# Head projections in two halves of 384 weight columns instead of three units of 256, with other ring sizes, on one core

## The chip, the cores and the metric

The program runs on one core of one Trainium2 chip. The metric is the device time of one execution in microseconds; of the kernel before there are three runs. The profile's own execution is a fourth, and its times count from its first instruction.

## What is computed

One step of a hybrid decoder layer for 512 prompt tokens and 8 x 4 sample tokens, width 1024. The part that the change touches is the input projection of the four attention heads and what is done with it:

```python
z_q, z_k, z_v, z_conv, z_mq, z_gate = split_combined(h @ lw['w_in'])
q, k, v = attention_qkv(z_q, z_k, z_v, pos, lw)        # norm of each head vector, rotary on 32 of 128 dims
for g, (window, dilation) in enumerate(((128, 1), (512, 4), (2048, 16))):
    o, l = dilated_band_attention(q[:, :, g * 4:(g + 1) * 4], k, v, window, dilation)
a = combine_dilated(outs, lses).reshape(B, S, ATTN_WIDTH) @ lw['w_attn_proj']
m = memory_branch(z_mq, mem_k, mem_v, lw)              # attention of normed z_mq over 256 memory tokens
out = merge_branches(z_gate, a, conformer, m, lw['w_out'])
y = x1 + hier_moe(rms_norm(x1))                        # 32 experts, top 1 group, top 2 in it
```

Each head h thus has six vectors of 128 per token out of `w_in`: Q0, Q1, Q2 (one for each window), K, V and MQ (the query into the memory). The weights are float32; the kernel multiplies them in three passes of a rounded high part and a low part.

## The kernel before

The stages follow each other: memory keys and values (`mem_kv`), the four heads, three convolution units (`glu`), the sample tokens' attention, the branches and gates, the output projection, the router, and 32 experts. Within the heads the code is written as `project_head(0)`, then for each h `attend_head(h)` and `project_head(h + 1)`. A scheduler then sets the order of the instructions on each engine, and each engine keeps to its order.

**Projection.** A head's weights come as three units of 256 columns (`cols_h`: Q0 Q1, then Q2 K, then V MQ), each a 1 MB block of a ring in SBUF. `split` makes the high part by a cast on ACT (L231) and the low part by a subtraction on DVE (L232), into the pool `whl`. For each unit the four blocks of 128 tokens are multiplied by `mm_nat` (L238 to L240, 24 matmuls of 256 columns each, called projection matmuls here), and two blocks share a PSUM tile of `mm`, which has three tiles. Then `norm_vecs` squares on ACT (L368), takes the root on POOL (L370, L371) and scales on DVE (L373); `rope` rotates on POOL; TensorE transposes (L441, L460) into a tile of `tr`, and a copy brings the result to `T`. `sample()` (L400 to L414) multiplies the 32 sample tokens by all three units and uses one `mm` tile and one `tr` tile; its last copy, on ACT (L406), needs DVE's norm.

**Attention.** For each of four query blocks: scores (L480 to L488) from the Qs and K, exp (L492), transposes (L498, L499), copies (L501 on DVE, L502 on ACT), values (L505, L508), a scaling on ACT (L510), a transpose (L512) and a copy (L513, ACT). Then twice, for the memory: scores (L518), exp (L525), scaling (L529), transposes (L533), a copy (L535, DVE), values (L538), a copy (L540, ACT). The pool `tr` has two PSUM tiles, and they go round in the order of the code: `attend_head(h)` takes all its turns before the transposes of `project_head(h + 1)`.

**Loads.** SP issues the weight loads; a load waits until its block is free and, by its semaphore, until the transfer eight issues before it has landed. The expert stage takes its 1 MB blocks from several pools in turn: `ring` 6, `ring2` 4, `ring2b` 2, `ring2c` 1, `ring3` 4, `ring4` 2, `ring5` 2, together 21; a load (L573) waits for the matmuls that read the block before: gate (L1477, `pg`), up (L1477, `pu`) and down (L1495, `pd`). An expert has six blocks.

## Time and profile before

| | before |
|---|---|
| runs, us | 1236.84, 1236.11, 1234.14 |
| median, us | 1236.11 |
| profiled execution, span, us | 1233.3 |
| PE busy, us (share) | 1157.4 (94%) |
| DVE, ACT, POOL busy, us | 483.4, 302.5, 290.2 |

The span is what the profile records from the first to the last instruction; the profile gives no time for what lies around it, and the median of the three runs is 2.8 us above the span. A busy engine has an instruction under way; PE is TensorE's matmuls. In the rows further down, a time stands from the span's start.

### The profile page before, as it was taken

To read this page: it belongs to the slowest core of one execution; us is meant where nothing else is said; L and a number is where in the kernel's file an instruction comes from. 1 tells how busy PE (TensorE), PEld (TensorE's weight loads), DVE (VectorE), ACT (ScalarE), POOL (GpSimd) and SP (SyncE) were. 2 spreads that over 40 slices of the span, in tenths; PEclk is the share of its full clock that TensorE was granted. 3 is DMA by queue.
4 is the path that set the end of the run, shared out by engine and by line. 5 is a ranking of instruction groups with operands and counts; after the bars stand their busy time and mean duration, and the time that the engine had idled before them with its cause. 6 is when DMAs were issued, how large, how long until landed. Compare 5 with 4: busy or idle time off the path is not lost. (4 is left out here: it accounts for less than half of the span.)

```text
span 1233.3 us, 22282 instructions
## 1 busy us (share of the span) xinstructions
PE 1157.4 (94%) x9248; PEld 850.2 (69%) x9250; DVE 483.4 (39%) x959; ACT 302.5 (25%) x731; POOL 290.2 (24%) x472
## 2 busy tenths in 40 slices
PE   6999999999999989999999988999999998898884
PEld 6898898989546889999998844555555554444441
DVE  6644434443635879856432263112142121111110
ACT  7434343422322422144332231000000000000000
POOL 5443434530840730213221000111111111111001
PEclk9999999999999989999999998999999999999998
DMA  9995754133647542312328487999999999999994
GB/s 319 228 330 153 228 164 139 43 108 103 239 137 266 184 150 69 103 44 95 137 74 358 154 305 297 388 394 399 401 393 400 397 394 401 403 407 401 402 399 145
DMA packets 125575, 313.02 MB, mean 254 GB/s; under 512 B 12842, under 2 KB 69490, under 8 KB 108833
## 3 DMA queue, kind: packets, MB, share of 16 engines
q1 hardware_dynamic: 115440, 295.58, 64.1%
q0 software_dynamic: 7280, 14.36, 5.2%
q10 hardware_dynamic: 2752, 1.65, 0.5%
q8 instruction: 74, 1.21, 0.4%
q14 instruction: 29, 0.23, 0.1%
HBM read 295.66 MB, written 31.35 MB: 265 GB/s over the span
## 5 line engine op out<-in xcount | busy, mean ns | idle before, releaser
L1499 POOL DMA_INDIRECT out_y_all<-work,ids x32 | 49.6, 1549 | 459.9 <-DVE work L1498 420.3
L664 PE MATMUL mm<-hTh,lo 128*128 128x272 f32 x512 | 148.6, 292 | 0.0
L662 PE MATMUL mm<-hTh,hi 128*128 128x272 f32 x512 | 148.6, 290 | 0.0
L663 PE MATMUL mm<-hTl,hi 128*128 128x272 f32 x512 | 148.5, 290 | 0.0
L1477 PE MATMUL pu<-w,xgT 128*64 128x256 f32 x992 | 115.6, 381 | 17.9 <-DMA w<-in_w_expert_up 16.6
L1495 PE MATMUL pd<-w,work 128*64 128x512 f32 x512 | 119.7, 609 | 1.4 <-DMA w<-in_w_expert_down 1.4
L1477 PE MATMUL pg<-w,xgT 128*64 128x256 f32 x992 | 115.0, 380 | 4.1 <-DMA w<-in_w_expert_gate 2.8
L1477 PEld LDWEIGHTS pu<-w,xgT 128*64 128x64 f32 x992 | 69.1, 137 | 61.2 <-DMA w<-in_w_expert_up 26.6
L238 PE MATMUL mm<-hi,hTh 128*128 128x256 f32 x384 | 110.2, 287 | 0.0
L239 PE MATMUL mm<-lo,hTh 128*128 128x256 f32 x384 | 110.0, 286 | 0.0
L240 PE MATMUL mm<-hi,hTl 128*128 128x256 f32 x384 | 109.8, 286 | 0.0
L1477 PEld LDWEIGHTS pg<-w,xgT 128*64 128x64 f32 x992 | 70.3, 137 | 55.7 <-issue 16.7
L232 DVE TENSOR_TENSOR lo<-w,hi 128x2048 fp32r<-128x2048 f32 (+2 forms) x46 | 82.2, 1803 | 45.9 <-ACT hi L231 45.8
L1486 DVE TENSOR_TENSOR work<-work,pu 128x256 f32<-128x256 f32 x32 | 13.5, 421 | 216.1 <-PE pu L1477 216.1
L662 PEld LDWEIGHTS mm<-hTh,hi 128*128 128x128 f32 x512 | 96.8, 189 | 1.8 <-ACT aS L896 0.8
L663 PEld LDWEIGHTS mm<-hTl,hi 128*128 128x128 f32 x512 | 97.0, 190 | 0.3 <-issue 0.2
L664 PEld LDWEIGHTS mm<-hTh,lo 128*128 128x128 f32 x512 | 96.5, 189 | 0.6 <-issue 0.5
L683 DVE SCALAR_TENSOR_TENSOR cT<-u,cT 128x512 f32<-128x512 f32 x120 | 89.8, 766 | 1.7
L1495 PEld LDWEIGHTS pd<-w,work 128*64 128x64 f32 x512 | 34.4, 139 | 65.1 <-issue 60.1
L1296 PE MATMUL px<-h,ohs 128*64 128x512 f16 x620 | 74.0, 380 | 5.6 <-DVE gates L1373 2.8
L231 ACT CAST hi<-w 128x2048 fp32r<-128x2048 f32 (+2 forms) x50 | 68.0, 1389 | 28.1 <-PE mm L663 24.7
L999 POOL TENSOR_TENSOR z<-z,gth 128x272 f32<-128x272 f32 x32 | 35.7, 1117 | 164.4 <-DVE gth L998 164.4
(452 smaller groups left out, 2114.1 us busy)
## 6 DMA issues: line engine op xcount, KB each, us to landing
w<-in_w_expert_gate SPq DMA_DIRECT2D x64, 1024.0 KB, 11.1
w<-in_w_expert_up SPq DMA_DIRECT2D x64, 1024.0 KB, 10.3
w<-in_w_expert_down SPq DMA_DIRECT2D x64, 1024.0 KB, 11.2
w<-in_w_in SPq DMA_DIRECT2D x30, 512.0 KB, 7.1
w<-in_w_in SPq DMA_DIRECT2D x12, 1024.0 KB, 6.9
out_k_win_sample<-in_cache_k SPq DMA_DIRECT2D x8, 1016.0 KB, 12.7
out_v_win_sample<-in_cache_v SPq DMA_DIRECT2D x8, 1016.0 KB, 14.8
w<-in_cache_k SPq DMA_DIRECT2D x6, 1024.0 KB, 5.8
```

Source lines behind the costliest of these rows:

```text
L231: nc.scalar.copy(hi[:, s], v8(t)[:, s])
L232: last_lo[0] = e.tensor_tensor(lo[:, s], v8(t)[:, s], hi[:, s].bitcast(F32), op=ALU.subtract)
L238: nc.tensor.matmul(ps, xh[k], wh[k], start=(k == 0), stop=False)
L239: nc.tensor.matmul(ps, xh[k], wl[k], start=False, stop=False)
L240: nc.tensor.matmul(ps, xl[k], wh[k], start=False, stop=(k == n - 1))
L662: nc.tensor.matmul(ps, wh[k], xh[k], start=(k == 0), stop=False)
L663: nc.tensor.matmul(ps, wh[k], xl[k], start=False, stop=False)
L664: nc.tensor.matmul(ps, wl[k], xh[k], start=False, stop=(k == n - 1))
L683: nc.vector.scalar_tensor_tensor(cTf[:, c, :NP], u[:, c, j:j + NP], w, cTf[:, c, :NP], op0=ALU.mult, op1=ALU.add)
L1296: nc.tensor.matmul(px[CAP * f:CAP * f + CAP], oh[:, i, :], src[:, 4 * f:4 * f + 4, :], start=(i == GORD[0] and r == 0), stop=(i == GORD[-1 ...
L1477: last = nc.tensor.matmul(ps[CAP * f:CAP * f + CAP], xT[:, k, :], ws[k // 4][:, k % 4, 256 * f:256 * f + 256], start=(k == 0), stop=(k == 7))
L1495: last = nc.tensor.matmul(pd[CAP * f:CAP * f + CAP], hT[:, kk % 2, CAP * (kk // 2):CAP * (kk // 2) + CAP], w[4 + kk // 2][:, kk % 2, 512 * ...
```

## The change

`project_head` makes two passes over the token blocks, each with 384 weight columns: half 0 takes all of unit 0 and the first 128 columns of unit 1 (Q0, Q1, Q2), half 1 the rest of unit 1 and all of unit 2 (K, V, MQ). The new `split3` writes the high and low parts of a half into tiles of 384 columns; they make `whl` larger, and the six blocks of `ring3`, which stand in its place later, use that room. A PSUM tile of `mm` now holds one token block of a half. There are 768 projection matmuls of 384 columns where there were 1152 of 256. `sample()` of head 0 stands at the start of half 1. The ring has five blocks instead of six, `ring3` six instead of four, so the expert stage has 22 instead of 21. The scratch for DMA descriptors is 4 KB. Lines of the changed file are shifted: L238 is L253, L368 L383, L400 L415, L406 L421, L413 L428, L510 L520, L512 L522, L513 L523, L525 L535, L533 L543, L535 L545, L538 L548, L540 L550; the transposes of the queries are now L468, those of K and MQ L461.

```diff
@@ -47,14 +47,14 @@
 
 TCKW = dict(schedule_with_timeline_sim=True)
 
-RING = 6
+RING = 5
 RING2 = 4
 RING2B = 2
 RING2C = 1
-RING3 = 4
+RING3 = 6
 RING4 = 2
 RING5 = 2
-SPOS = 2
+SPOS = 4
 NPG = 2
 COJ = 1
 WK = {4: "hi", 5: "lo"}
@@ -65,7 +65,7 @@
 DEPTH = 4
 NBUSY = (50, 4)
 GORD = (4, 0, 1, 2, 3)
-ORD3 = (0, 3, 1, 2)
+ORD3 = (0, 4, 5, 1, 2, 3)
 AHJ = 1
 NGH = 3
 MVT = {0: "hi"}
@@ -230,6 +230,21 @@
             s = slice(q * n, q * n + n)
             nc.scalar.copy(hi[:, s], v8(t)[:, s])
             last_lo[0] = e.tensor_tensor(lo[:, s], v8(t)[:, s], hi[:, s].bitcast(F32), op=ALU.subtract)
+        return hi, lo
+
+    def split3(units, half, n):
+        hi = whl.tile([P, 8, 384], F32R, name=nm("hi"), tag="hi")
+        lo = whl.tile([P, 8, 384], F32R, name=nm("lo"), tag="lo")
+        if half == 0:
+            parts = ((units[0], 0, 0, 256), (units[1], 0, 256, P))
+        else:
+            parts = ((units[1], P, 0, P), (units[2], 0, P, 256))
+        for q in range(n):
+            ks = slice(q * 8 // n, (q + 1) * 8 // n)
+            for t, c, d, w in parts:
+                src = v8(t)[:, ks, c:c + w]
+                nc.scalar.copy(hi[:, ks, d:d + w], src)
+                nc.vector.tensor_tensor(lo[:, ks, d:d + w], src, hi[:, ks, d:d + w].bitcast(F32), op=ALU.subtract)
         return hi, lo
 
     def mm_nat(ps, xh, xl, wh, wl):
@@ -385,9 +400,9 @@
     ropec = rope_t[:, 0:P].rearrange("p (i c) -> p i c", i=4)
     ropes = rope_t[:, P:2 * P].rearrange("p (i c) -> p i c", i=4)
 
-    def bc4(v, ip):
+    def bcn(v, ip, n):
         w = v[:, 2 * ip:2 * ip + 2, :]
-        return w.unsqueeze(2).to_broadcast([P, 2, 2, 32])
+        return w.unsqueeze(2).to_broadcast([P, 2, n, 32])
 
     def project_head(h, units):
         T = t_tile(nm("T")).bitcast(F32).rearrange("p (s t) -> p s t", s=5)
@@ -413,52 +428,47 @@
                 nc.tensor.transpose(psT[:, c * 96:(c + 1) * 96], sA[:96, c, :], ident[:96, :96])
             nc.vector.tensor_copy(Ts[:, h].rearrange("p a q -> p (a q)"), psT[:, :192])
 
-        for u in range(3):
-            wh, wl = split(units[u], H0ENG if h == 0 else (nc.vector,))
-            for ip in range(2):
-                if u * 2 + ip == (SPOS if h == 0 else 0):
+        al = slice(None)
+        for half in range(2):
+            wh, wl = split3(units, half, 2 if h == 0 else 1)
+            for i in range(4):
+                if half * 4 + i == (SPOS if h == 0 else 0):
                     sample()
-                ps = mm.tile([P, 2, 2, HD], F32, name=nm("mm"), tag="mm")
-                for i2 in range(2):
-                    i = 2 * ip + i2
-                    s = slice(i * P, (i + 1) * P)
-                    mm_nat(ps[:, i2], [hTh[:, k, s] for k in range(8)], [hTl[:, k, s] for k in range(8)],
-                           [wh[:, k, :] for k in range(8)], [wl[:, k, :] for k in range(8)])
-                A = hs_.tile([P, 2, 2, HD], F32, name=nm("A"), tag="A", bufs=3)
-                al = slice(None)
-                if u < 2:
-                    ix = [(al, i2, s_, al) for i2 in range(2) for s_ in range(2)]
-                    gg = [gq, gq if u == 0 else gk] * 2
-                    norm_vecs(ps, A, [(x, x) for x in ix], gg, P)
-                    rope(A, bc4(ropec, ip), bc4(ropes, ip), [P, 2, 2])
-                    if u == 1:
-                        nc.gpsimd.dma_start(
-                            O["k_win_prompt"][0, 0, ip * 256:(ip + 1) * 256, h, :].rearrange("(i p) d -> p i d", p=P),
-                            A[:, :, 1, :])
+                ip, i2 = i // 2, i % 2
+                ps = mm.tile([P, 3, HD], F32, name=nm("mm"), tag="mm")
+                s = slice(i * P, (i + 1) * P)
+                mm_nat(ps.rearrange("p s d -> p (s d)"), [hTh[:, k, s] for k in range(8)],
+                       [hTl[:, k, s] for k in range(8)], [wh[:, k, :] for k in range(8)], [wl[:, k, :] for k in range(8)])
+                if i2 == 0:
+                    A = hs_.tile([P, 2, 3, HD], F32, name=nm("A"), tag="A", bufs=3)
+                if half == 0:
+                    norm_vecs(ps, A, [((al, v), (al, i2, v)) for v in range(3)], [gq] * 3, P)
+                else:
+                    nc.scalar.copy(vh[:, i, :], ps[:, 1, :])
+                    VENG.dma_start(vp[32 * i:32 * i + 32], vh[:, i, :])
+                    norm_vecs(ps, A, [((al, 2 * v), (al, i2, v)) for v in range(2)], [gk, gmq], P)
+                if i2 == 0:
+                    continue
+                nv = 3 - 2 * half
+                rope(A[:, :, :nv], bcn(ropec, ip, nv), bcn(ropes, ip, nv), [P, 2, nv])
+                if half:
+                    nc.gpsimd.dma_start(
+                        O["k_win_prompt"][0, 0, ip * 256:(ip + 1) * 256, h, :].rearrange("(i p) d -> p i d", p=P),
+                        A[:, :, 0, :])
                     pt = tr.tile([P, 2, 2, P], F32, name=nm("tr"), tag="tr")
-                    for i2 in range(2):
-                        for s_ in range(2):
-                            nc.tensor.transpose(pt[:, i2, s_, :], A[:, i2, s_, :], ident)
-                    dst = T[:, 2 * u:2 * u + 2, ip * 256:(ip + 1) * 256].rearrange("p s (i t) -> p s i t", i=2)
-                    for s_ in range(2):
-                        dv, sv = dst[:, s_], pt[:, :, s_]
-                        if (u, s_) != (1, 1):
-                            dv = dv.rearrange("p i (r a) -> p i r a", r=4)
-                            sv = sv.rearrange("p i (a r) -> p i r a", r=4)
-                        if u == 0:
-                            nc.scalar.copy(dv, sv)
-                        else:
-                            nc.vector.tensor_copy(dv, sv)
-                else:
-                    nc.scalar.copy(vh[:, 2 * ip:2 * ip + 2, :], ps[:, :, 0, :])
-                    for i in range(2 * ip, 2 * ip + 2):
-                        VENG.dma_start(vp[32 * i:32 * i + 32], vh[:, i, :])
-                    ix = [(al, i2, 1, al) for i2 in range(2)]
-                    norm_vecs(ps, A, [(x, x) for x in ix], [gmq, gmq], P)
-                    pt = tr.tile([P, 2, P], F32, name=nm("tr"), tag="tr")
-                    for i2 in range(2):
-                        nc.tensor.transpose(pt[:, i2, :], A[:, i2, 1, :], ident)
-                    nc.scalar.copy(T[:, 4, ip * 256:(ip + 1) * 256].rearrange("p (i t) -> p i t", i=2), pt)
+                    for j in range(2):
+                        for v in range(2):
+                            nc.tensor.transpose(pt[:, j, v, :], A[:, j, v, :], ident)
+                    dst = T[:, 3:5, ip * 256:(ip + 1) * 256].rearrange("p s (i t) -> p i s t", i=2)
+                    (nc.scalar.copy if ip else nc.vector.tensor_copy)(dst, pt)
+                    continue
+                for j in range(2):
+                    pt = tr.tile([P, 3, P], F32, name=nm("tr"), tag="tr")
+                    for v in range(3):
+                        nc.tensor.transpose(pt[:, v, :], A[:, j, v, :], ident)
+                    q0 = (2 * ip + j) * P
+                    dst = T[:, 0:3, q0:q0 + P].rearrange("p s (r a) -> p s r a", r=4)
+                    (nc.scalar.copy if j else nc.vector.tensor_copy)(dst, pt.rearrange("p s (a r) -> p s r a", r=4))
         nc.gpsimd.dma_start(O["v_win_prompt"][0, 0, :, h, :].rearrange("(i p) d -> p i d", p=P), vh)
         return T, vh, vp
 
@@ -1627,7 +1637,7 @@
     from concourse.bass_utils import run_bass_kernel_spmd
 
     arrs, cols = _consts()
-    nc = bacc.Bacc("TRN2", target_bir_lowering=False, num_devices=1)
+    nc = bacc.Bacc("TRN2", target_bir_lowering=False, num_devices=1, dynamic_dma_scratch_size=4096)
     arrays, ins, outs = {}, {}, {}
     named = [(k, np.ascontiguousarray(inputs[k])) for k in _INS] + list(zip(_CONSTS, arrs))
     for k, a in named:
```

TensorE, end of the attention of head 1, as it stood before. `tr` tiles are the attention's, `mm` tiles those of the projection of head 2 (`hi`, `lo` weights, `hTh` tokens), `P` the probabilities of the memory part, `sA` the sample tile.

```order
L512 MATMUL tr_1984<-ident,PT_1973 128x128 [waits Activation_49]
L533 MATMUL tr_2000<-ident,P_1992 128x128 [waits PE_49]
...
L239 MATMUL mm_2324<-lo_2245,hTh 128x256
...
L238 MATMUL mm_2404<-hi_2400,hTh 128x256
...
L538 MATMUL tr_2007<-PT_2005,mv 128x256 [waits DVE_49,Activation_49]
...
L533 MATMUL tr_2024<-ident,P_2016 128x128 [waits PE_49]
...
L239 MATMUL mm_2404<-lo_2401,hTh 128x256
...
L538 MATMUL tr_2031<-PT_2029,mv 128x256 [waits DVE_49,Activation_49]
...
L413 MATMUL tr_2090<-ident,sA_2073 128x96 [waits PE_49,Pool_49]
...
L239 MATMUL mm_2470<-lo_2401,hTh 128x256
```

The rows left out between these are projection matmuls of head 2 or further transposes of the same group: 5 and 22 of them stand between the first transposes of L533 and the first L538, 26 and 7 between the second ones, and 23 follow the transposes of L413 before anything that waits.

The same place now. `mm_2226` is the last tile of the projection of head 2, `mm_2539` the first of head 3, `A` the normed queries of head 2.

```order
L255 MATMUL mm_2226<-hi_2098,hTl 128x384
...
L518 MATMUL tr_1802<-vp_1252,PT_1799 32x128 [waits DMAHW0_49,Activation_49]
...
L522 MATMUL tr_1810<-ident,PT_1799 128x128 [waits Activation_49]
L543 MATMUL tr_1826<-ident,P_1818 128x128 [waits PE_49]
...
L548 MATMUL tr_1833<-PT_1831,mv 128x256 [waits DVE_49,Activation_49]
...
L543 MATMUL tr_1850<-ident,P_1842 128x128 [waits PE_49]
...
L548 MATMUL tr_1857<-PT_1855,mv 128x256 [waits DVE_49,Activation_49]
...
L428 MATMUL tr_1918<-ident,sA_1901 128x96 [waits PE_49,Pool_49]
...
L468 MATMUL tr_2000<-ident,A_1947 128x128 [waits Activation_49,Pool_49]
...
L468 MATMUL tr_2005<-ident,A_1947 128x128 [waits DVE_49]
...
L253 MATMUL mm_2539<-hi_2487,hTh 128x384 [waits Activation_49]
```

Left out are 24 sample matmuls of head 3 (L415, between the first two rows shown), score masks, the transposes of the last block, and repeats of the rows shown; no projection matmul stands between the first row and the last.

ACT at that place now: the squares of the last projection tile, the high parts for half 1 of head 3, then the attention's copies and exponentials.

```order
L447 COPY vh_1868<-mm_2226 128x128 [waits PE_49]
L383 ACTIVATE sq_2254,hms_2253<-mm_2226 128x128 [waits Pool_49]
L246 CAST hi_2715<-w_2278 128x8x128 [waits DMAHW4_49]
L246 CAST hi_2715<-w_2281 128x8x256 [waits DMAHW2_49,DMAHW1_49]
L448 DMA vp_1869<-vh_1868 32x4x128 [waits DMAHW0_49,Activation_49]
L383 ACTIVATE sq_2254,hms_2253<-mm_2226 128x128 [waits Activation_49]
L523 COPY aT_613<-tr_1773 128x4x32 [waits PE_49]
L535 ACTIVATE P_1842,den_1841<-S_1837,m_1840 128x256 [waits PE_49]
L535 ACTIVATE P_1842,den_1841<-S_1837,m_1840 128x256
L512 COPY PT_1799<-tr_1795 128x128 [waits DVE_49]
```

Before, the cast of a unit stood between squares of earlier tiles, with projection matmuls still to come on TensorE; now both casts of a half stand behind the last projection tile of the head and ahead of four operations of the attention's tail.

SP's order of loads at the start, before. `w_195`, `w_198` and `w_201` are the three units of head 0, `w_193` the last unit of the memory keys and values; `cf`, `gmq`, `cm` and `br` stand for twenty small loads.

```order
L219 DMA w_193<-in_w_mem_kv 128x8x256 [waits DMAHW0_49]
L219 DMA w_195<-in_w_in 128x8x128 [waits DMAHW1_49]
L581 DMA cf<-in_constf 128x306 [waits DMAHW3_49]
...
L593 DMA gmq<-in_mq_norm_g 128x128 [waits DMAHW7_49]
...
L219 DMA w_198<-in_w_in 128x8x128 [waits DMAHW3_49,DVE_49,Pool_49]
...
L600 DMA cm<-in_constm 128x1504 [waits DMAHW0_49]
...
L652 DMA br<-in_b_router_expert 128x32 [waits DMAHW0_49]
L219 DMA w_201<-in_w_in 128x8x128 [waits DMAHW1_49,DVE_49,Pool_49]
```

The same place now.

```order
L219 DMA w_193<-in_w_mem_kv 128x8x256 [waits DMAHW0_49]
L591 DMA cf<-in_constf 128x306 [waits DMAHW1_49]
...
L603 DMA gmq<-in_mq_norm_g 128x128 [waits DMAHW5_49]
...
L219 DMA w_195<-in_w_in 128x8x128 [waits DMAHW3_49,DVE_49,Pool_49]
...
L610 DMA cm<-in_constm 128x1504 [waits DMAHW6_49]
...
L662 DMA br<-in_b_router_expert 128x32 [waits DMAHW6_49]
L219 DMA w_198<-in_w_in 128x8x128 [waits DMAHW7_49,DVE_49,Pool_49]
...
L219 DMA w_201<-in_w_in 128x8x128 [waits DMAHW1_49,DVE_49,Pool_49]
```

The first unit now stands behind ten small loads, and the second, which half 0 needs too, stands behind all twenty, next to the third.

## Rows read from the trace of the kernel before

**Rows 1.** The page: busy time (share of the span), and one costly group.

```profile
PE 1157.4 (94%) x9248; PEld 850.2 (69%) x9250; DVE 483.4 (39%) x959; ACT 302.5 (25%) x731; POOL 290.2 (24%) x472
...
L1499 POOL DMA_INDIRECT out_y_all<-work,ids x32 | 49.6, 1549 | 459.9 <-DVE work L1498 420.3
```

**Rows 2.** Windows: length, busy us (count) by engine, PEclk, DMA share, GB/s.

```profile
60.00:300.00 240.00, 240.00 (x2184) 213.41 (x2176) 99.62 (x258) 94.64 (x332) 94.45 (x174) 1.00 0.52 164
740.00:1018.00 278.00, 267.39 (x2060) 144.00 (x2058) 66.81 (x148) 22.77 (x43) 29.53 (x19) 0.99 1.00 385
1018.00:1233.00 215.00, 173.26 (x1264) 85.62 (x1264) 31.84 (x58) 11.06 (x23) 20.05 (x13) 0.98 0.94 366
```

**Rows 3.** Timeline of PE: start, length, instruction; 48 steps between the second and third row.

```profile
42.87 0.28 PE L238 MATMUL mm<-hi,hTh 128*128 128x256 f32 x1
...
76.93 0.28 PE L238 MATMUL mm<-hi,hTh 128*128 128x256 f32 x1
...
82.63 0.28 PE L238 MATMUL mm<-hi,hTh 128*128 128x256 f32 x1
...
564.94 0.28 PE L662 MATMUL mm<-sh,ph 128*128 128x272 f32 x1
...
567.94 0.29 PE L663 MATMUL mm<-hTl,hi 128*128 128x272 f32 x1
```

**Rows 4.** Timeline of PE: an attention tail and sample matmuls, projection rows left out.

```profile
125.94 0.60 PE L533 MATMUL tr<-ident,P 128*128 128x128 f32 x4
...
129.59 1.02 PE L538 MATMUL tr<-PT,mv 128*128 128x256 f32 x4
...
130.45 0.60 PE L533 MATMUL tr<-ident,P 128*128 128x128 f32 x4
...
204.70 1.49 PE L400 MATMUL mm<-w,hTs 128*32 128x256 f32 x18
```

**Rows 5.** ACT by line and shape, 140 to 260 (last row 30 to 45).

```profile
L231 ACT CAST hi<-w 128x2048 fp32r<-128x2048 f32 x7 | 13.3, 1900 | 0.0
L368 ACT ACTIVATE sq<-mm 128x128 bf16<-128x128 f32 x42 | 11.7, 279 | 2.3 <-PE mm L240 1.7
...
L525 ACT ACTIVATE P<-S,m 128x256 f32<-128x256 f32 x8 | 3.7, 471 | 0.0
...
L513 ACT COPY aT<-tr 128x128 f32<-128x128 f32 x8 | 3.1, 388 | 21.0 <-PE tr L512 21.0
...
L510 ACT ACTIVATE PT<-tr,m 128x128 f32<-128x128 f32 x8 | 2.9, 368 | 11.4 <-PE tr L508 11.3
...
L231 ACT CAST hi<-w 128x1024 fp32r<-128x1024 f32 x4 | 4.0, 1048 | 0.0
```

**Rows 6.** DVE by line and shape, 140 to 260.

```profile
L232 DVE TENSOR_TENSOR lo<-w,hi 128x2048 fp32r<-128x2048 f32 x7 | 16.1, 2293 | 10.2 <-ACT hi L231 10.2
...
L373 DVE SCALAR_TENSOR_TENSOR A<-mm,hrs,gq 128x128 f32<-128x128 f32 x26 | 8.0, 344 | 16.5 <-PE tr L441 8.8 <-POOL hrs L371 7.7
...
L535 DVE COPY PT<-tr 128x512 f32<-128x512 f32 x4 | 2.8, 688 | 4.4 <-PE tr L533 4.4
```

**Rows 7.** DMA issues of SP in time, then landing of the pair at 33.28.

```profile
17.75 6.96 SPq L219 DMA_DIRECT2D w<-in_w_in  x2
...
33.28 1.02 SPq L219 DMA_DIRECT2D w<-in_w_in  x2
...
45.51 14.54 SPq L219 DMA_DIRECT2D w<-in_w_in  x8
...
DMA to landing us min/median/max: 4.1/4.8/5.4
```

**Rows 8.** DMA issues of SP, expert weights.

```profile
736.66 13.90 SPq L573 DMA_DIRECT2D w<-in_w_expert_gate  x2
...
843.19 3.25 SPq L573 DMA_DIRECT2D w<-in_w_expert_gate  x2
...
943.21 4.01 SPq L573 DMA_DIRECT2D w<-in_w_expert_gate  x2
```

## The prediction

> **What bounds the kernel now.** The page's busy times come first: PE is busy for 1157.4 us of the span of 1233.3 [rows 1]. The windows by stage say what that share hides. [...] From 740 on the DMA share is 1.00, and from 1018 PE works only 173 of 215 us: there the expert weights set the end [rows 2]. Their issue by SP shows where this begins: the pair of gate loads at 736.66 takes 13.90 us, since its second load waits for a block; from 750.6 on load follows load, and the six experts between the gate loads at 843.19 and those at 943.21 are 36 blocks of 1 MB in 100.0 us, 2.78 each [rows 8]. The loads up to there are limited by how many blocks are free, the rest by the DMA.
>
> A shift of the heads is passed on in full: SP's loads at 736.66 wait for the expert matmuls, and these follow the heads on the same engine. The end is then the time of that wait plus the blocks still to be loaded.
>
> **The matmuls.** The page's mean of a projection matmul is its latency; what counts is the distance from start to start. 48 steps of 256 columns take 82.63 − 76.93 = 5.70 us, 0.1188 each; 24 steps of 272 columns take 567.94 − 564.94 = 3.00, 0.1250 each [rows 3]. So 16 columns more cost 6.2 ns, 0.39 a column; and 0.1188 less 256 × 0.39 leaves some 19 ns that do not depend on the columns. [...] Before: 1152 × 0.1188 = 136.9 us. [...] I take **−6.0 us**. [...]
>
> [...]
>
> **The tails of the attention.** This is the term that decides. Before, K came with the second of three units; after it there was a third unit and the next head's first to work on, and the tail of `attend_head(h)` was spread among projection matmuls: in the trace the first memory transposes stand at 125.94, the matmuls that need their copy only at 129.59, the next transposes at 130.45 [rows 4], with PE never idle. Now K comes with the last half. The scores start later against the next head's projection, and the order of TensorE shows the result: between the last projection matmul of head 2 and the first of head 3 there stands the tail of head 1's attention and only the 24 sample matmuls as other work. The projection of head 3 can't go ahead of it, since its matmuls stand behind in the order, and the tail is a chain over PE, ACT and DVE.
>
> Its length from the end of the last projection matmul, by the new order: on ACT a copy and a square (0.39 + 0.28), the two casts of half 1 (1.05 + 1.90), another square 0.3, a copy 0.39, two exponentials with their sums (0.47 + about 0.2 each), a copy of 0.3 [rows 5]: 6.0. Then four small matmuls, taken at 0.4, the scaling 0.37 [rows 5], the transpose and the first memory transposes 0.8: 7.6. The copy 0.69 [rows 6], matmuls 0.86 (130.45 − 129.59), transposes 0.6 [rows 4], copy 0.69, matmuls 0.86: 11.3. The sample's transposes and copy, about 0.6, two norms of 0.34 [rows 6] and the copy that frees the PSUM tile, 0.3: 12.9. PE has this to do meanwhile: the sample matmuls, 48 records at (1.49 − 0.38) / 17 = 0.065, 3.1 us; two groups of transposes and two of matmuls, 2 × (0.6 + 0.86) [rows 4]; and about 1.3 for the small matmuls and the other transposes: 7.3. PE loses 12.9 − 7.3 = 5.6.
>
> Between heads 1 and 2 the order leaves the fourth query block before the end; the chain is squares and casts 3.9, the subtraction 2.29 that stands on DVE ahead of the second copy [rows 6], that copy 0.69, matmuls 0.86, and the sample's 1.6: 9.3, with 6.3 of work: 3.0. Between head 3 and the convolution there is one cast instead of two, 24 convolution matmuls (24 × 0.125 = 3.0) take the place of the sample's, and two more groups of transposes come behind: 12.1 against 8.5, 3.6. The tail of head 3's attention lies among convolution matmuls as before. Together **+12.2**. Bounds: +6, if half of it finds cover that I don't see (the hand-overs and copies overlap more); +19, if POOL adds to it: the order sets eight issues of sample DMAs ahead of the rotation of K for head 2.
>
> **The start.** Half 0 of head 0 needs units 0 and 1. Before, unit 0 was issued from 17.75 on, unit 1 at 33.28, landing 4.1 to 5.4 us later, unit 2 at 45.51 [rows 7], and the first projection matmul of head 0 ran at 42.87 [rows 3]. Between the second and the third pair SP had twelve small loads: 12.2 us, because each waits for the transfer eight issues earlier. Now unit 0 is behind ten small loads (it takes the place of the pair at 33.28 without 1 MB ahead of it, 2.8 us earlier: 30.5, landed by 35.9), and unit 1 behind ten more. At the old pace that is 30.5 + 12.2 = 42.7; with the smaller backlog I take 39, landing by 44.4; a cast and a subtraction of half the piece add about 1.7: 46.1, against 42.87: **+3.3**. Bounds +1 and +7.
>
> **The expert blocks.** 22 instead of 21: one more block is loaded before the wait at 736.66, so one fewer after it: **−2.8** [rows 8]; bounds −2.8 and 0.
>
> **The rest, at nothing.** A ring of five instead of six in the middle stages: the DMA share of 0.52 [rows 2] leaves room for a block that is asked for later; if a load is late where PE waits, it costs up to its 2.8 us, twice perhaps: 0 to +6. The scratch of 4 KB: it could hold up the scatters of the experts, but POOL waits 459.9 us in front of these 32 for its input [rows 1], so there is slack but for the last one: 0 to +2; no row shows a wait for descriptors. More squares, roots and copies on POOL and ACT: both are under half busy from 60 to 300 [rows 2].
>
> **Sum.** −6.0 + 12.2 + 3.3 − 2.8 = +6.7: the profiled execution would go from 1233.3 to 1240.0. The median of the runs lies 2.8 us above that span; from it, 1236.1 + 6.7 = **1243**. A measurement of this kernel can tell about 0.2%, 2.5 us, from no change.
>
> **Rivals.**
> - *The tails stay covered.* It is the same place, with another reading: if PE's queue works on through the tail with less than 3 us lost in all, the rest, −6.0 − 2.8 + 3.3 = −5.5, wins: about 1232. For it: before, the same chain cost nothing, and the scheduler set this order too. Against it: no projection matmul stands between these rows any more. The point from which it decides is 2.9 us lost (faster by 0.2%); from 7.9 on the kernel is slower by more than 0.2%. Chance 0.22.
> - *The two cancel*, with 3 to 8 us lost in the tails, within 2.5 us of before: 0.10.
> - *Wide matmuls cost less than their columns.* If each column beyond 256 cost half of the 0.39 ns of [rows 3], a matmul would take 0.144 and the projections 768 × 0.144 = 110.9, a saving of 26 instead of 6: 1223 with the tails as forecast. [...] Chance 0.03. [...]
> - *A late load on top*: in the ring of five, or at the start (the bound of +7), 6 to 10 us more: about 1251. For it, SP's queue is strictly in order; against it, the DMA share of 0.52. Chance 0.08.
>
> **How the numbers follow.** The forecast itself has 0.57: slower by 0.2 to 1.1%. Slower in all 0.57 + 0.08 = 0.65, same 0.10, faster 0.22 + 0.03 = 0.25. The range has to take in most of the covered case and of the late one: 1229 to 1254; the forecast alone 1239 to 1249.
>
> **What would show it.** Idle time of PE, some 3 to 6 us, at each of three places between projections, ended by ACT and DVE (the copies of L545, L550, L421), where there was none. [...] The first projection matmul of head 0 near 46. One load more before SP's long wait for the expert matmuls, and the same 2.78 us per block behind it. Wrong would be a PE that is busy throughout the heads, or a long wait of SP in the middle stages.

## The result and the profile after

The median is 1243.34 us (1242.63 to 1243.63) against 1235.72 of the kernel before, timed beside it: a ratio of 1.0067, 95% interval 1.0053 to 1.0081. The profiled span is 1240.8 us, 7.5 more than before. The forecast of 1243 holds in the sum. Of its terms only some hold, and terms that it did not have nearly cancel: a low clock at the start and a longer wait of SP on one side, a shorter end of the program on the other.

The page first, then the windows of the heads and of the two parts of the expert stage (length, busy us by engine, PEclk, DMA share, GB/s), as in [rows 1, 2].

```profile
PE 1160.0 (93%) x8864; PEld 847.9 (68%) x8866; DVE 485.5 (39%) x960; ACT 301.1 (24%) x732; POOL 293.6 (24%) x488
```

```profile
60.00:300.00 240.00, 233.03 (x1777) 202.57 (x1776) 98.25 (x248) 91.71 (x328) 97.79 (x194) 1.00 0.49 153
760.00:1030.00 270.00, 260.19 (x2020) 140.76 (x2018) 59.84 (x138) 17.81 (x37) 29.56 (x19) 0.99 1.00 383
1030.00:1240.00 210.00, 175.48 (x1282) 86.88 (x1276) 32.67 (x60) 11.62 (x24) 20.04 (x13) 0.99 0.98 379
```

In the heads PE now idles 6.97 us where it idled none. The waits of PE in that window (us in total, times, longest) have the three copies that were forecast among them (L545, L550, L421):

```profile
PE tr L548 <- DVE PT L545: 4.5, 5, 0.9
PE tr L468 <- ACT mT L550: 1.2, 3, 0.4
PE tr L522 <- ACT PT L520: 0.7, 2, 0.5
PE tr L468 <- DVE T L471: 0.4, 1, 0.4
PE mm L253 <- ACT vS L421: 0.2, 1, 0.2
```

The timeline of PE shows them between heads 2 and 3: from the last projection matmul of head 2 to the first of head 3 it is 13.1 us (12.9 in the forecast); masks, sample matmuls and more of the tail stand where lines are left out. The last line is the window of that place: PE is busy for 10.43 us of it.

```profile
199.25 0.34 PE L255 MATMUL mm<-hi,hTl 128*128 128x384 f32 x1
...
205.75 0.33 PE L522 MATMUL tr<-ident,PT 128*128 128x128 f32 x1 [0.49 <-ACT PT L520]
...
207.39 1.10 PE L548 MATMUL tr<-PT,mv 128*128 128x256 f32 x4 [0.87 <-DVE PT L545]
...
209.87 1.10 PE L548 MATMUL tr<-PT,mv 128*128 128x256 f32 x4 [0.94 <-DVE PT L545]
...
211.53 0.84 PE L468 MATMUL tr<-ident,A 128*128 128x128 f32 x6 [0.39 <-ACT mT L550]
212.39 0.44 PE L253 MATMUL mm<-hi,hTh 128*128 128x384 f32 x1
```

```profile
199.25:212.39 13.14, 10.43 (x95) 6.43 (x95) 7.11 (x12) 7.13 (x22) 4.65 (x5) 1.00 0.79 264
```

The idle time of the three places is 1.5 us (near 152), 2.7 (here) and 2.8 (near 268). That is below the 3 to 6 us that the prediction named as its sign.

The start and the pace, from the same view; before, the first of these stood at 42.87 [rows 3].

```profile
46.70 1.01 PE L253 MATMUL mm<-hi,hTh 128*128 128x384 f32 x2 [3.94 <-ACT hi L246]
...
49.55 0.52 PE L255 MATMUL mm<-hi,hTl 128*128 128x384 f32 x1
49.87 0.52 PE L253 MATMUL mm<-hi,hTh 128*128 128x384 f32 x1
...
52.76 0.35 PE L253 MATMUL mm<-hi,hTh 128*128 128x384 f32 x1
52.95 0.34 PE L254 MATMUL mm<-lo,hTh 128*128 128x384 f32 x1
...
246.04 0.34 PE L253 MATMUL mm<-hi,hTh 128*128 128x384 f32 x1
...
249.54 0.34 PE L255 MATMUL mm<-hi,hTl 128*128 128x384 f32 x1
```

```profile
47.00:52.00 5.00, 5.00 (x21) 4.56 (x21) 3.55 (x6) 2.43 (x6) 1.07 (x2) 0.50 1.16 297
```

The wait of 3.94 us is the late weight. Behind it the granted clock is 0.50 (the third column from the right in the window of 47 to 52) up to 52.8: the rows at 49.55 and 49.87 lie 0.32 apart. From 246.04 to 249.54 there are 20 steps: 0.175 each.

SP's loads answer to [rows 7, 8]: the first unit of head 0 at 30.06, the next two from 39.75 on; then the last load before the long wait, the first behind it, and a place in the middle of the expert stage.

```profile
30.06 1.02 SPq L219 DMA_DIRECT2D w<-in_w_in  x2
...
39.75 17.36 SPq L219 DMA_DIRECT2D w<-in_w_in  x8
...
746.21 2.07 SPq L583 DMA_DIRECT2D w<-in_w_expert_gate  x2
761.49 2.76 SPq L583 DMA_DIRECT2D w<-in_w_expert_up  x2
...
913.50 14.47 SPq L583 DMA_DIRECT2D w<-in_w_expert_down  x2
928.06 0.89 SPq L583 DMA_DIRECT2D w<-in_w_expert_gate  x2
```

Up to the long wait 26 loads are issued, 25 before, as forecast. The pair at 913.50 takes 14.47 us: between its two loads SP reads the count of overflow blocks (L1586; it sets how often the loop behind the experts runs), which waits for tables that DVE makes. The waits of SP's queue, first that of before, then those of after with the one at the program's end, then the end of before:

```profile
SPq L1576 <- DVE w L1531: 5.4, 1, 5.4
```

```profile
SPq L1586 <- DVE w L1541: 12.9, 1, 12.9
...
SPq L1648 <- PEq L1648: 2.0, 2, 1.4
```

```profile
SPq L1638 <- PEq L1638: 8.1, 2, 7.5
```

The last pair is the barrier at the end. What stands in it is POOL's last long DRAIN instruction, which the trace records apart from the busy rows: 7.10 us before, 1.02 after.

So the 7.5 us are: the sample stage begins 12.2 later (322.91 against 310.70), the first `pd` matmul 11.3 later (757.77, 746.50), from there to the last weight load it takes 460.8 us instead of 458.4 (+2.5), and the DRAIN is 6.1 shorter: 11.3 + 2.5 − 6.1 = 7.7, within rounding of the 7.5.

### The profile page after: what moved, and what is told of

It reads as the page before. It is cut to its first block, busy times and chain, and to the rows that moved or that the text cites. A ratio compares the mean times of both kernels' runs of the same rounds, so it can differ in the third digit from the quotient of the medians.

```text
span 1240.8 us, 21529 instructions
## 1 busy us (share of the span) xinstructions
PE 1160.0 (93%) x8864; PEld 847.9 (68%) x8866; DVE 485.5 (39%) x960; ACT 301.1 (24%) x732; POOL 293.6 (24%) x488
## 5 line engine op out<-in xcount | busy, mean ns | idle before, releaser
L253 PE MATMUL mm<-hi,hTh 128*128 128x384 f32 x256 | 89.6, 351 | 4.1 <-ACT hi L246 3.9
L255 PE MATMUL mm<-hi,hTl 128*128 128x384 f32 x256 | 88.8, 347 | 0.0
L254 PE MATMUL mm<-lo,hTh 128*128 128x384 f32 x256 | 88.2, 345 | 0.0
L1495 ACT ACTIVATE work<-pg 128x256 f32<-128x256 f32 x32 | 12.3, 383 | 251.1 <-PE pg L1487 251.1
L232 DVE TENSOR_TENSOR lo<-w,hi 128x2048 fp32r<-128x2048 f32 (+1 forms) x31 | 54.5, 1777 | 28.7 <-ACT hi L231 28.7
## 6 DMA issues: line engine op xcount, KB each, us to landing
w<-in_w_expert_gate SPq DMA_DIRECT2D x64, 1024.0 KB, 11.2
w<-in_w_expert_down SPq DMA_DIRECT2D x64, 1024.0 KB, 11.2
out_v_win_sample<-in_cache_v SPq DMA_DIRECT2D x8, 1016.0 KB, 14.5
```

The source lines that it names most:

```text
L232: last_lo[0] = e.tensor_tensor(lo[:, s], v8(t)[:, s], hi[:, s].bitcast(F32), op=ALU.subtract)
L253: nc.tensor.matmul(ps, xh[k], wh[k], start=(k == 0), stop=False)
L254: nc.tensor.matmul(ps, xh[k], wl[k], start=False, stop=False)
L255: nc.tensor.matmul(ps, xl[k], wh[k], start=False, stop=(k == n - 1))
```

## Experiments

Medians, each beside the kernel before on the same chip; the other columns are from the profiled execution (us): first projection matmul of head 0, first transpose of the sample stage, first `pd` matmul, issue of the last expert load, POOL's last long DRAIN. These columns come from one execution each, and the executions of one run lie up to 5.9 us apart (start2: 1233.40 to 1239.27).

| run | median | before | ratio, 95% interval | head 0 | sample | `pd` | last load | DRAIN |
|---|---|---|---|---|---|---|---|---|
| before | | | | 42.87 | 310.70 | 746.50 | 1204.9 | 7.10 |
| the change | 1243.34 | 1235.72 | 1.0067 (1.0053–1.0081) | 46.70 | 322.91 | 757.77 | 1218.6 | 1.02 |
| own_tile | 1237.88 | 1234.11 | 1.0025 (1.0016–1.0035) | 46.58 | 315.70 | 754.95 | 1214.2 | 0.81 |
| kv_first | 1252.90 | 1234.11 | 1.0146 (1.0130–1.0163) | 48.95 | 337.12 | 775.25 | 1232.2 | 0.85 |
| start_room | 1245.15 | 1234.11 | 1.0084 (1.0067–1.0101) | 42.70 | 323.43 | 761.61 | 1221.9 | 1.02 |
| novf_late | 1238.52 | 1234.11 | 1.0033 (1.0021–1.0044) | 47.31 | 323.18 | 760.74 | 1217.4 | 1.02 |
| start2 | 1237.09 | 1234.80 | 1.0018 (1.0006–1.0030) | 42.65 | 316.31 | 753.28 | 1213.2 | 1.02 |
| combo2 | 1227.92 | 1234.80 | 0.9944 (0.9927–0.9961) | 42.49 | 310.02 | 747.40 | 1203.8 | 0.81 |
| units_ring5 | 1237.95 | 1234.80 | 1.0028 (1.0016–1.0040) | 42.76 | 312.54 | 747.27 | 1213.0 | 0.85 |
| before_novf_late | 1235.55 | 1234.80 | 1.0005 (0.9994–1.0015) | 43.12 | 310.95 | 745.65 | 1204.0 | 7.10 |
| units_scratch | 1228.39 | 1233.96 | 0.9953 (0.9937–0.9970) | 42.71 | 310.54 | 746.33 | 1204.5 | 0.85 |
| units_best | 1225.73 | 1233.96 | 0.9933 (0.9916–0.9949) | 42.79 | 310.62 | 745.28 | 1200.9 | 0.85 |
| scratch8 | 1231.18 | 1234.36 | 0.9971 (0.9960–0.9981) | 42.66 | 310.49 | 747.29 | 1205.7 | 1.87 |

The change was timed beside a kernel before of 1235.72, the other runs beside one of 1233.96 to 1234.80. What is said below of a run against the change is the difference of the medians. Taken against the kernel before beside each, the gains over the change are smaller: own_tile 3.9 us instead of 5.5, start2 5.3 instead of 6.2, novf_late 3.2 instead of 4.8, combo2 14.5 instead of 15.4; start_room is 3.4 slower instead of 1.8, kv_first 11.2 instead of 9.6. Each goes in the same direction either way.

**own_tile.** A PSUM tile for the projections' and the sample's transposes alone, and two tiles for the scores instead of three.

```diff
-    sps = heads.enter_context(pool("sps", 3, PSUM))
+    sps = heads.enter_context(pool("sps", 2, PSUM))
+    trp = heads.enter_context(pool("trp", 1, PSUM))
...
-            psT = tr.tile([P, 512], F32, name=nm("tr"), tag="tr")
+            psT = trp.tile([P, 512], F32, name=nm("trp"), tag="trp")
...
-                    pt = tr.tile([P, 3, P], F32, name=nm("tr"), tag="tr")
+                    pt = trp.tile([P, 3, P], F32, name=nm("trp"), tag="trp")
```

> The changed kernel, but the transposes of the projections and of the sample tokens have a PSUM tile of their own (one), and the scores two tiles instead of three. In the order of TensorE the tails of the attention then lie among projection matmuls again. Theory (the heads lose 8.0 us in bare tails: 12.2 in all, less 3.8 of a later start, less 2.9 of a low clock after it, plus 2.5 saved by wide matmuls): the idle time of TensorE from 60 to 300 us falls from 7.0 to under 1.5 us, the sample stage starts 6 to 8 us earlier (322 to 324 instead of 329.6), and the run takes 1235 to 1237 instead of 1243.3. Rival (the loss of the heads is in the wide matmuls or in the small instructions themselves, whatever stands between them): 1241 to 1244. Second rival: two tiles for scores instead of three make new waits and the run is no faster.

The window of the heads:

```profile
60.00:300.00 240.00, 240.00 (x1834) 208.43 (x1833) 101.97 (x257) 95.14 (x336) 100.36 (x194) 1.00 0.49 152
```

No idle time is left, the sample stage begins 7.2 us earlier (its first score matmul, at 329.63 in the changed kernel, at 322.82), and the run is 5.5 faster; 4.4 of the 7.2 are lost again before the first expert, the largest piece at 443.8, where PE waits 3.85 us for a copy of POOL (the kernel before waits 4.36 there, the changed one does not) and the clock is 0.83 in the 20 us around it. By estimate 1.2 of the 7.2 us are not the tile's: behind the wait at the start the clock is back at 1.00 from 50.4 on in this trace, from 52.8 on in the change's, and half of these 2.4 us is lost. The time misses the theory's 1235 to 1237 by 0.9, but its mechanism holds: the tails were bare because the next transposes queued behind them in the same two tiles.

**kv_first.** `for turn, half in enumerate((1, 0))`, the units loaded in the order 2, 1, 0.

> The changed kernel with its halves in the other order: K, V and MQ in the first pass, the three queries in the second, weights loaded in that order. The prediction said that the tails are bare because K comes with the last half. If that is the cause, K is now early and the run takes 1235 to 1237. Rival: what counts is that the transposes of the last half, whatever they hold, queue behind the attention's tail in the same two PSUM tiles; the order of TensorE shows the tails bare at the same three places, and the run stays within 2.5 us of 1243.3.

The tails stay bare at the same three places, though K comes first. But the queries come last now, and each score needs those too, so this run alone can't part the two readings; own_tile does. The run is worse than either theory said, 9.6 us above the change. Its profiled execution is the slowest of its four (1255.96; the others 1252.40 to 1252.98). In it the heads start 2.3 later, and there is a new wait of PE, with a low clock behind it, and a low clock in the third tail (last line), where no wait is longer than 0.97 us. Why ACT is late at 118.73 no run shows.

```profile
118.73 0.65 PE L518 MATMUL tr<-vp,PT 32*32 32x128 f32 x8 [3.35 <-ACT PT L512]
```

```profile
120.00:125.00 5.00, 5.00 (x17) 5.00 (x17) 2.15 (x9) 1.15 (x5) 1.91 (x5) 0.50 0.92 231
276.00:285.00 9.00, 7.22 (x23) 5.29 (x23) 2.34 (x5) 0.74 (x3) 0.00 (x0) 0.50 0.17 64
```

**start_room, start2.** First the token and sample tiles out of the ring; then (start2, the second part of the diff) also the router's loads, of which one is shown, behind the third unit.

```diff
-    xs += [loadx(x_src[i], "x2", i - 2, lambda n: raw()) for i in range(2, 4)]
+    xs += [loadx(x_src[i], "x2", i - 2, lambda n: npl.tile([P, 2 * D], F32, name=n, tag="x2", bufs=1)) for i in range(2, 4)]
...
-            nc.sync.dma_start(wr[:, :, 0:4], I["w_router_group"][0].rearrange("(k p) g -> p k g", p=P))
+            with tc.issue_after(w0_last.ins):
+                nc.sync.dma_start(wr[:, :, 0:4], I["w_router_group"][0].rearrange("(k p) g -> p k g", p=P))
```

> The changed kernel, but token tiles 2 and 3 and the sample tokens are loaded outside the ring of five, so that the first unit of head 0 needs no freed block and stands in front of the small loads in SP's order again. Theory: the start costs 3.8 us of waiting and 2.9 us more, since the 11 matmuls after the wait run at 0.32 us instead of 0.175 and the granted clock is 0.50 from 46 to 52.7; with the weights there in time the first projection matmul of head 0 runs at 43 to 44, the clock stays at 1.00, and the run takes 1236 to 1238. Rival: the wait moves to the second unit, which half 0 needs too (first matmul at 45 or later, clock low again): 1241 to 1243.

> The kernel of the run with room at the start, with one more edit: the seven router loads and the constants stand behind the third unit of head 0 in SP's order, not in front of it. In the run before, the first unit was in time (first projection matmul at 42.7) but ACT sat 8.0 us in its order on the cast of the third unit, issued at 44.4, and TensorE waited 4.2 us at 56.6. Theory (the start of the changed kernel is a late weight unit, whichever half 0 or 1 needs): issued at about 36.5 the third unit has landed by 45, no wait of more than 1 us remains before 60 us, the clock stays at 1.00 there, and the heads end at 314.5 to 317 instead of 322.9; the run takes 1236 to 1238. Rival: the wait moves once more (tokens, gains, the next head's units): 1241 to 1245.

In start_room the wait moved, to where neither theory had it, and the time lies above both. The rows are of PE, of ACT, and of SP, whose six loads begin with the two of the third unit:

```profile
56.58 1.11 PE L358 MATMUL tr<-ident,x 128*128 128x128 f32 x4 [4.21 <-DVE mkT L574]
```

```profile
52.49 1.99 ACT L246 CAST hi<-w 128x1024 fp32r<-128x1024 f32 x2 [7.96 <-DMA w<-in_w_in]
```

```profile
44.38 9.56 SPq L219 DMA_DIRECT2D w<-in_w_in  x6
```

ACT sat on the cast for half 1, DVE behind it, and a transpose of tokens behind DVE's copy. In start2 the third unit is in time too, PE is never idle at the start and keeps its clock:

```profile
40.00:60.00 20.00, 20.00 (x129) 19.43 (x128) 11.87 (x22) 9.21 (x30) 6.50 (x13) 1.00 0.89 211
```

The sample stage begins 6.6 us earlier, the run is 6.2 faster: as the theory said.

**novf_late, before_novf_late.** In both kernels:

```diff
-    n_ovf = nc.values_load(novf[0:1, 0:1], min_val=0, max_val=MAXOVF)
+    with tc.issue_after(loads[-1]):
+        n_ovf = nc.values_load(novf[0:1, 0:1], min_val=0, max_val=MAXOVF)
```

> The changed kernel, but SP reads the count of overflow blocks behind its last weight load instead of in the middle of the expert loads. Theory: the 12.9 us that SP waits there for DVE's tables (5.4 before the change) leave the DMA engines without work for about 5 us; without the wait the loads run on at 2.78 us each, the last values matmul comes 4.5 to 6 us earlier, and the run takes 1237 to 1239. Rival: the loads issued ahead cover the wait, or the DMA gives the time back behind it: within 1.5 us of 1243.3.

> The kernel before, with SP's read of the overflow count behind its last weight load. SP waits 5.4 us there in the kernel before, and the loads issued ahead may cover it. Theory (an SP wait costs what it exceeds the loads under way, which is about 6 to 8 us as the 12.9 us of the changed kernel cost 4.8): within 1.5 us of the kernel before, 1233 to 1235. Rival: a wait of SP costs in proportion: 2 us faster.

Windows at the wait, of the changed kernel and of novf_late (the last two columns are DMA share and GB/s):

```profile
920.00:925.00 5.00, 5.00 (x50) 3.34 (x48) 2.29 (x11) 0.38 (x1) 1.54 (x1) 1.00 0.74 195
925.00:930.00 5.00, 4.64 (x42) 2.59 (x39) 4.83 (x19) 0.58 (x1) 0.00 (x0) 1.00 0.23 57
```

```profile
920.00:925.00 5.00, 5.00 (x44) 2.92 (x42) 0.87 (x2) 0.12 (x1) 1.54 (x1) 1.00 1.02 419
925.00:930.00 5.00, 5.00 (x50) 3.05 (x48) 4.83 (x23) 0.26 (x1) 0.00 (x0) 1.00 1.06 369
```

From the first `pd` to the last load it is 456.6 us instead of 460.8, and the run is 4.8 faster. The trace shows only this stage of the gain: its execution is the slowest of the eight (1242.78), and from the sample stage to the first `pd` it takes 2.7 us more than the change's, where nothing was edited. In the kernel before, the same edit changes nothing (458.3, 458.4). A wait of 5.4 us lay under the loads already under way, one of 12.9 did not. It grew because the tables' scratch is a block of `ring`: in the trace DVE begins them at 907.1 before, behind a down matmul (`pd`), and at 923.5 after, behind a gate matmul (`pg`):

```profile
907.14 0.42 DVE L1522 TENSOR_TENSOR w<-cn,cf 128x256 f32<-128x256 f32 x1 [1.19 <-PE pd L1495]
```

```profile
923.46 0.43 DVE L1532 TENSOR_TENSOR w<-cn,cf 128x256 f32<-128x256 f32 x1 [2.70 <-PE pg L1487]
```

So the block that the tables take has another reader, and it frees later. That the turn of five and 22 blocks did this is read from the order; no run took that part alone.

**combo2.** All three repairs together.

> The changed kernel with all three edits: a PSUM tile of their own for the projections' transposes, the loads of the start in time, the count of overflow blocks read behind the last load. If the three losses are separate (5.5 and 4.8 us as measured alone, about 6 at the start), their sum of 16 brings 1243.3 to 1226 to 1229, below the kernel before. Rival: behind the heads part of what is won is lost again (the run with a tile of its own ended its heads 7.2 us earlier and its first expert only 2.8): 1230 to 1235.

It is 15.4 us below the change and 0.56% below the kernel before. The three single gains add up to 16.5 (12.4 against 14.5, each taken against the kernel before beside it): within that uncertainty the losses are separate.

**units_ring5.** `RING = 5`, scratch 4 KB, units of 256 columns.

> The kernel before (three units of 256 columns) with a ring of five and the scratch of 4 KB, ring3 as before: 20 expert blocks. The prediction set the ring and the scratch at nothing in the middle stages and an expert block at 2.8 us. By that: the heads end at 310.7 within 1.5 us, though the first unit is issued some 12 us later (half of it would be needed later too), one block fewer costs 2.8, the run takes 1237 to 1240. Rival: the ring of five itself costs the start (first projection matmul after 45, clock low behind it): 1242 to 1246. Second rival: the place of the scratch tile for the overflow tables in the ring changes, and SP's wait for the count with it: up to 6 us either way.

The sample stage begins 1.8 later (PE waits 1.74 us at 50.76), so the ring was not quite free; from the first `pd` to the last load it is 465.7 us, 7.3 more than before, of which a block explains 2.8. For the rest there are two waits of SP between two loads at 932 to 945, for a block that an up matmul (`pu`) still reads and for the tables:

```profile
SPq L573 <- PE pu L1477: 6.4, 1, 6.4
SPq L1576 <- DVE w L1531: 4.8, 1, 4.8
```

No run took either of them away in this kernel. The median lies where forecast only because the DRAIN gave 6.2 back, which was not expected here.

**units_scratch, scratch8.** `dynamic_dma_scratch_size=4096` or `8192` in the kernel before, nothing else.

> The kernel before with the DMA scratch of 4 KB and nothing else; the order of instructions on every engine is that of the kernel before. The prediction set the scratch at 0 to +2 us. In the runs so far POOL's last DRAIN, for which the other engines wait at the end, takes 7.1 us in the two kernels with the old scratch and 0.8 to 1.0 us in the eight with 4 KB. Theory (the scratch sets the length of that DRAIN): 0.85 to 1.0 again, the span 6.1 us shorter, the run 1228 to 1230 against 1234.8. Rival (the DRAIN goes by what was scattered last, or by the ring of five): 7.1 and no difference, within 1.5 us.

> [...] With 4 KB POOL's last DRAIN took 0.85 us, with the default 7.1. Theory (the DRAIN grows with the scratch, in proportion between these two): about 2.9 us, the run about 4 us faster than the kernel before, 1229 to 1231. Rival (a step: a scratch that has never been filled once round by the scatters drains quickly, or the other way): 0.9 or 7.1 us, and the run at 1228 or at 1234.

SP's wait in the final barrier, with 4 KB and with 8:

```profile
SPq L1638 <- PEq L1638: 1.8, 2, 1.3
```

```profile
SPq L1638 <- PEq L1638: 2.8, 2, 2.3
```

The scratch alone makes the kernel before 5.6 us faster. The DRAIN takes 0.85 us at 4 KB, 1.87 at 8 KB and 7.10 at the default. That is no step, and 1.87 is not the theory's 2.9 either. The 2.9 needs the size of the default, which no run shows; so how the DRAIN goes from 8 KB to the default is open.

**units_best.** Units of 256 columns, scratch of 4 KB, `RING3 = 5` (22 blocks), the count read late.

> The kernel before, with three units of 256 columns, the scratch of 4 KB, the room that this frees as a fifth block of ring3 (22 blocks in all), and the overflow count read behind the last load. By the terms as measured: 6.1 us less at the end, 2.8 less for the block, nothing for the count: 1234.8 - 8.9 = 1226, within 2.5 us of the halves with their three repairs (1227.9), so that the halves themselves would be worth nothing. Rival: the block brings nothing (its load is hidden, or the wait moves): 1228 to 1230.

As forecast, and the fastest of all: 2.7 us below units_scratch for the one block. It has the 22 blocks, the scratch and the late count of combo2, without the halves, and is 2.2 us faster than it (1.4 when each is taken against the kernel before beside it): repaired, the halves gain nothing over the units.

**split_wide.** In `project_head`, two matmuls, of 256 and of 128 columns, for each of 384. Its projections come out with other values, so it is no kernel to use; it is read for its distances and up to the sample stage alone (median 1272.47, before 1233.96).

```diff
+                        for c0, c1 in ((0, 256), (256, 384)):
+                            nc.tensor.matmul(pf[:, c0:c1], xa[:, k, s], wa[:, k, c0:c1],
```

> The changed kernel, each projection matmul of 384 columns written as two, of 256 and of 128, into the same PSUM tile: 1536 instead of 768. Measured so far: 0.1190 us from start to start at 256 columns, 0.1751 at 384. Theory (about 0.007 us for each matmul besides its columns, by the line through these two): 0.063 at 128, a pair 0.182, the heads 5 us longer, the run 1247 to 1250. Rival (a matmul of 128 columns costs much more than the line says, since its weights of 128 rows are loaded each time): a pair 0.2 or more, the heads 19 us longer or more, 1260 or above.

Pairs in the timeline of PE, 16 steps from the third row to the last:

```profile
59.70 0.22 PE L444 MATMUL mm<-hi,hTh 128*128 128x128 f32 x1
59.76 0.40 PE L444 MATMUL mm<-lo,hTh 128*128 128x256 f32 x2
59.99 0.39 PE L444 MATMUL mm<-hi,hTl 128*128 128x256 f32 x2
...
63.67 0.39 PE L444 MATMUL mm<-hi,hTh 128*128 128x256 f32 x2
```

A pair takes 0.230, not 0.182: the rival's price holds. If the piece of 256 columns costs its 0.119, the piece of 128 costs 0.111, not 0.063. The starts divide the pair in another way: the next pair starts 0.06 behind the short piece (59.70 to 59.76), and the short piece 0.17 behind the wide one. PE's weight loads, one for each piece, start 0.108 and 0.122 us apart in turn (means of 761 and 696 distances), so two of them fill the pair; that they are what holds it up is argued from this, not shown. The sample stage begins at 353.61.

## Why the forecast came out as it did

| term | forecast | measured | from |
|---|---|---|---|
| matmuls | −6.0 | −2.6 | 768 × 0.1751 − 1152 × 0.1190 |
| tails, rest of the heads | +12.2 | +8.4 | start2: (316.31 − 42.65) − (310.70 − 42.87) + 2.6 |
| start | +3.3 | +6.6 | change against start2: 322.91 − 316.31 |
| expert loads | −2.8 | +2.5 | first `pd` to last load |
| scratch, rest | 0 | −6.1, −0.9 | DRAIN; sample stage to first `pd` |
| sum | +6.7 | +7.9 | span: +7.5 |

- **The matmuls: the size was off.** No run shows the −6.0 of the sum; the measured distances give −2.6. The line through 256 and 272 columns, by estimate from [rows 3], gives 0.169 at 384; 665 distances under 0.2 us of the run give 0.1751. The 19 ns "that do not depend on the columns" are some 7 ns by the line through 0.1190 and 0.1751, and split_wide shows that this line does not reach down to 128 columns. The rival of cheap wide matmuls falls by the measured 0.1751 too, against its 0.144.
- **The tails: the mechanism was right, the size nearly twice too large.** Place, chain (13.1 against 12.9) and the waits came as forecast. But PE's idle time is 6.97 us in all: between heads 2 and 3 PE is busy for 10.4 of the 13.1 us, and the forecast counted 7.3. The 8.4 of the table is a remainder. Of it 6.1 go with the tile of own_tile, in traces without a wait at the start (first projection matmul to sample stage: 267.5 us in combo2, 273.7 in start2). The other 2.3 stay when the tails are covered: combo2's 267.5 are only 0.3 below the 267.8 of the kernel before, where the matmuls alone save 2.6. No run names these 2.3. Its reason, "K comes with the last half", is too narrow: kv_first has K first and bare tails, and own_tile has K last and no idle time of PE.
- **The start: one term was missing.** The wait came as forecast (46.70 against 46.1). That the clock falls behind a wait of 3.9 us, and 6.06 us of work run at a clock of 0.50 (by estimate half of them, 3.0, lost), was not in the sum. The price changes with the execution: behind the same wait in own_tile (3.82 us) the clock is low for 3.4 us. That the twelve small loads between 33.28 and 45.51 [rows 7] each waited for an earlier transfer is not shown: in the trace of the kernel before the profile shows no wait of SP's queue there.
- **The expert blocks: the block is right, the queue was missed.** One block is worth 2.7 to 2.8 us (units_best, 26 loads for 25). But I did not follow the load of the count through SP's order, nor ask which block the tables' scratch would get; novf_late puts that at 4.2 us in this stage.
- **The rest at nothing: wrong for the scratch.** It was bounded at 0 to +2 by the scatters' slack; no gain was thought of, since I looked for waits in the middle and not at the barrier at the end.

The errors cancel, and that is luck: the forecast was near by its sum, not by its parts. The halves themselves, repaired (combo2), begin the sample stage 0.7 us earlier than the units did; of the 6.9 us that combo2 gains over the kernel before, 6.3 are the DRAIN's (7.10 to 0.81).

## What to carry to other kernels

Before work is regrouped into larger pieces, ask what the last piece holds: where the next stage needs something from every piece, its chain starts after the last one, and the work that follows can fill it only if it does not queue for the same buffers; here a tile of its own was enough. A wait of 3.2 to 4.9 us on TensorE cost itself here, and 3.1 to 6.5 us of work behind it ran at a granted clock of 0.50. Follow every value read and every small load through SP's queue, where one read waited 12.9 us here, and look at the last microseconds of the trace by themselves: here a smaller scratch was worth 5.6 us there.

## What the hardware showed

- POOL's DRAIN at the end, with the same 32 scatters, takes 0.85 us with a scratch of 4 KB, 1.87 with 8 KB and 7.10 with the default, in the kernel before; in the changed kernel and its variants, all with 4 KB, it takes 0.81 to 1.02. The end of the program waits for it: SP's longest wait in the final barrier is 7.5 us in the kernel before, 2.3 with 8 KB, 1.3 with 4 KB, and 1.4 in the changed kernel.
- Matmuls with weights of 128 columns, from start to start: 0.119 us at 256 columns, 0.175 at 384, 0.230 for a pair of 256 and 128 (split_wide). Between 256 and 384 a column costs 0.44 ns. In the pair the weight loads start 0.108 and 0.122 us apart.
- From 30 us on, each of the 18 waits of PE of 3.2 to 4.9 us in these traces was followed by a granted clock of 0.50 for 3.1 to 6.5 us (6.1 us at 46.70 in the changed kernel, 3.4 at 46.58 in own_tile, 6.5 at 118.73 in kv_first). So was, a little later, each of the 14 waits of 2.8 us just ahead of the experts (739.44 before: 0.50 from 744.9 to 751.7). Behind shorter ones it went both ways: it fell behind 1.75 us at 432.93 in the changed kernel and stayed at 1.00 behind 1.74 at 50.76 in units_ring5.
- In the tails of the changed kernel, with waits of under 1 us, the clock stayed at 1.00; in the third tail of kv_first it was 0.50 from 275.4 to 285.6 though no wait there was longer than 0.97 us.
